# Split weights in one tile, the odd tiles of the contraction 128 bytes further, activations at one distance behind them

## The chip, the core and the metric

The kernel runs on one core of a Trainium2 chip. The time is device microseconds from launch to end; the kernel before takes 1659.15 us (median of three runs, 1659.05 to 1659.46). A core has a matrix engine (PE, TensorE) that reads its operands from on-chip memory (SBUF, 128 partitions wide) and adds its products up in PSUM; DVE (VectorE) and ACT (ScalarE) for elementwise work; POOL (GpSimd); and SP, which here issues the weight loads. Each engine runs its own list of instructions in order. Engines wait for one another on semaphores: an instruction counts one up when it is done, and another instruction is held until the count has reached a number.

## What is computed

One inference step of a decoder layer, for 256 prompt tokens and 8 x 4 sample tokens together, 288 columns. Cut to what matters here, it is a row of products of the tokens with large float32 weights:

```
proj = x @ w_in                        # 2048 -> 11280 columns
y_a  = (gB * conv3(gC * h)) @ w_a_out  # short convolution mixer
y_b  = gated_delta_rule(q, k, v, g, beta) normalised, * silu(z), @ w_b_out
x    = layer_norm(ALPHA * x + (sig(m_a) * y_a + sig(m_b) * y_b) @ w_o)
hid  = square(relu(x @ w_up))          # 2048 -> 8192
x    = layer_norm(ALPHA * x + hid @ w_down)
```

The outputs are the new x of both groups of tokens and the new states of the two convolutions and of the delta rule.

## The kernel before

Float32 products are made out of three matmuls of a shorter format (`float32r`): a weight w is split into `hi` = w rounded and `lo` = w - hi, the activations likewise, and PE adds up hi x hi, hi x lo and lo x hi.

All weights stream from memory in **blocks** of 512 KB: KB = 4 tiles of the contraction (k, 128 rows each) by GW = 256 columns, in SBUF 4096 bytes a partition. There are 496. Block i goes through four steps:

- `load(i)` (L167): SP fetches it into a `raw` buffer;
- `split_hi(i)` (L183): one ACT cast raw -> `hi`, 1024 elements a partition, line L187;
- `split_lo(i)` (L189): one DVE subtraction raw - hi -> `lo`, recorded under L142, the line of the helper `tt`;
- `matmuls(i)` (L196): for each of the four k, six matmuls of 288 columns: both 128-column halves c of `hi` with the high and the low activations (L219), then both halves of `lo` with the high activations (L221); 24 in a block.

`raw`, `hi` and `lo` come from a pool of four buffers each (L114), each buffer a tile of its own. The loop over the blocks (L1643 to L1734) writes the instructions out in a fixed order; nothing is reordered afterwards. From block 10 on, one turn of it is: `split_hi(i + 3)`, side work (a step of the delta rule up to the merge), `split_lo(i + 3)`, whatever falls due for finished groups (`due`, evacuations from PSUM), `matmuls(i)`, and the load of block i + 7. With four buffers, block i + 3 takes the buffers of block i - 1, so its cast must wait until PE has made its last `hi` matmul of block i - 1 and its subtraction until the last `lo` matmul; blocks i, i + 1 and i + 2 are split by then.

The activations lie in tiles of 16 rows (k) per partition, 288 float32 each, 1152 bytes from row to row: `xh`, `xl` for the input, `hh`, `hl` for the hidden layer, `ahl`, `mh`, `ml` for the mixers. `dh` and `dl`, the input of the up projection, have NX = 290 columns in a row, 1160 bytes, and `ohl` is allocated so too.

Taken from the built program, a weight tile before always starts 128 bytes past a multiple of 256, whichever k it is; an activation row of 1152 bytes starts in the same place for even k and 128 bytes from it for odd k, and the rows of `dh` and `dl` wander in steps of 136 bytes modulo 256.

Of the kernel before, what the change touches and what calls it, by code (L numbers as in the profile page):

```python
# [10 lines left out]
F32R = mybir.dt.float32r  # L11
# [5 lines left out]
P = 128  # L17
# [2 lines left out]
NS = 32  # L20
NT = NP_ + NS
NX = NT + 2
KT = D // P
H = 8
DFF = 8192
# [8 lines left out]
GW = 256  # L34
KB = 4
# [70 lines left out]
def hybrid_kernel(ctx: ExitStack, tc: tile.TileContext, A):  # L106
# [7 lines left out]
    wp = pool("wp", 4)  # L114
# [7 lines left out]
    def nm(s):  # L122
        counter[0] += 1
        return f"{s}{counter[0]}"
# [16 lines left out]
    def tt(out, a, b, op):  # L141
        dve.tensor_tensor(out=out, in0=a, in1=b, op=op)  # L142
# [8 lines left out]
    blocks = []  # L151
# [5 lines left out]
            blocks.append((gi, row0 + j * kb * P, j * kb, j == 0, j == nk // kb - 1))  # L157

    raw, his, los = {}, {}, {}
    due = {}  # L160
    fill = []

# [19 lines left out]

    def split_hi(i, step=KB):  # L183
        if i < len(blocks):
            his[i] = wp.tile([P, KB, GW], F32R, tag="hi", name=nm("hi"))
            for k in range(0, KB, step):
                act.copy(his[i][:, k:k + step], raw[i][:, k:k + step])  # L187

    def split_lo(i, step=KB):  # L189
        if i < len(blocks):  # L190
            los[i] = wp.tile([P, KB, GW], F32R, tag="lo", name=nm("lo"))
            r = raw[i] if blocks[i][0].get("by_token") else raw.pop(i)
            for k in range(0, KB, step):
                tt(los[i][:, k:k + step], r[:, k:k + step], his[i][:, k:k + step], SUB)

    def matmuls(i):  # L196
        gi, r0, k0, first, last = blocks[i]
        if gi.get("by_token"):
            return first_tokens(i, k0)
# [9 lines left out]
        h, l = (u.rearrange("p k c -> p (k c)").rearrange("p (k c) -> p k c", k=kb) for u in (h, l))  # L209
        for k in range(kb):  # L210
            xh_, xl_ = ah[:, k0 + k, 0:n], al[:, k0 + k, 0:n]
            st = first and k == 0
            en = last and k == kb - 1
            per = gi["cols"] // P // len(members)
            for u, m in enumerate(members):
                ts = [(m["ps"][:, t, 0:n], slice((per * u + t) * P, (per * u + t + 1) * P)) for t in range(per)]
                both = [(o, c, x) for o, c in ts for x in (xh_, xl_)]
                for o, c, x in both[::2] + both[1::2] if i == 0 else both:
                    pe.matmul(o, h[:, k, c], x, start=st and x is xh_, stop=False)  # L219
                for o, c in ts:  # L220
                    pe.matmul(o, l[:, k, c], xh_, start=False, stop=en)  # L221
# [12 lines left out]
    ph = {}  # L234
# [11 lines left out]
    ident = cst("ident")  # L246
    ones = cst("ones")

    xh = xp.tile([P, KT, NT], F32R, tag="XH", name="xh")
    xl = xp.tile([P, KT, NT], F32R, tag="XL", name="xl")  # L250
    hw = cp.tile([P, 24, 28], F32, name="hw")
# [165 lines left out]
    def wo_evac(p):  # L417
        q = slice(2 * p, 2 * p + 2)

        def resid(ps):  # L420
            pl = ph["pool"]
            if p == 0:
                ph["dl"] = pl.tile([P, KT, NX], F32R, tag="R3", name="dl")
                ph["dh"] = pl.tile([P, KT, NX], F32R, tag="R4", name="dh")
                t = ap_.tile([P, 2, H, NT], F32, tag="ao", name="lns").rearrange("p a h t -> p (a h) t")
                ph["qa"], ph["da"], ph["c"] = t[:, 0:2], t[:, 2:4], t[:, 4]
                ph["ln"] = [t[:, 5 + u] for u in range(4)]
                dh, dl = ph["dh"], ph["dl"]
                gbc = lnp[:, 0:32].rearrange("p (a k) -> p k a", a=2)
                act.copy(hmr, ones)  # L430
                act.copy(dh[:, :, NT:NX], gbc)
                tt(dl[:, :, NT:NX], gbc, dh[:, :, NT:NX], SUB)
            ph["s"] = pl.tile([P, 2, NT], F32, tag="yt", name=nm("s"), bufs=2)
            dd = ph["s"]
            stt(dd, xh[:, q, :], ALPHA, ps[:, :, 0:NT], MUL, ADD)
            stt(dd, xl[:, q, :], ALPHA, dd, MUL, ADD)
            if p:
                tt(dd, dd, bmid(ph["c"], 2), SUB)

        def centre(ps):  # L440
            tt(ph["c"], ph["s"][:, 0, :], ph["s"][:, 1, :], ADD)
            ph["chl"] = high_low(ph["c"], "sg")

        def shift(ps):
            cps = gtile()
            dd = ph["s"]
            row_sums(cps[:, 0:NT], ph["chl"])
            act.mul(ph["c"], cps[:, 0:NT], 1.0 / 256)
            tt(dd, dd, bmid(ph["c"], 2), SUB)

        def scaled(ps):
            dd, qa, da = ph["s"], ph["qa"], ph["da"]
            sd = ph["pool"].tile([P, 2, NT], F32, tag="sg", name=nm("sd"), bufs=2)
            for u in range(2):
                k = 2 * p + u
                dve.tensor_scalar(out=sd[:, u, :], in0=dd[:, u, :], scalar1=lnp[:, k:k + 1], scalar2=None, op0=MUL)
            act.copy(ph["dh"][:, q, 0:NT], sd)
            tt(ph["dl"][:, q, 0:NT], sd, ph["dh"][:, q, 0:NT], SUB)

        def sums(ps):  # L460
            dd, qa, da = ph["s"], ph["qa"], ph["da"]
            if p == 0:
                act.activation(qa, dd, AF.Square)
                act.copy(da, dd)
# [267 lines left out]
    def products(out, b, j, ks=range(KB)):  # L732
        h, l = kept[j]
        c = slice(b * P, b * P + P)
        for k in ks:
            kk = KB * j + k
            en = kk == KT - 1
            for x, w, stop in ((ph["hh"], h, False), (ph["hh"], l, False), (ph["hl"], h, en)):
                pe.matmul(out, x[:, kk, c], w[:, k, :], start=False, stop=stop)  # L739

    def first_tokens(i, k0):
        kept.append((his.pop(i), los.pop(i)))
# [849 lines left out]
    aux = []  # L1592
    steps = x_steps(0, 1)
    t0, o0 = steps[0]()
    his[0] = wp.tile([P, KB, GW], F32R, tag="hi", name=nm("hi"))
    los[0] = wp.tile([P, KB, GW], F32R, tag="lo", name=nm("lo"))
    t, h0, l0 = raw.pop(0), his[0], los[0]

    def split_first(k):
        for u in (2 * k, 2 * k + 1):  # L1600
            act.copy(h0[:, u], t[:, u])  # L1601
            tt(l0[:, u], t[:, u], h0[:, u], SUB)

    def turns(ts):
        for g in ts:
# [14 lines left out]
    turns(t0[0:2])  # L1620
    xs_out = x_sample(0)
    warm_up(1, 2)
    act.copy(h0[:, 0], t[:, 0])
    o0[0](dve.tensor_copy)
    xs_out()
    tt(l0[:, 0], t[:, 0], h0[:, 0], SUB)
    act.copy(h0[:, 1], t[:, 1])
    tt(l0[:, 1], t[:, 1], h0[:, 1], SUB)
# [14 lines left out]
    for i in range(len(blocks)):  # L1643
# [48 lines left out]
        if i == mark["merge"]:  # L1692
            gcm.__exit__(None, None, None)
            p3 = pool("p3")
            ph["pool"] = p3
            r1 = p3.tile([P, KT, NT], F32R, tag="R1", name="ahl")
            r4 = p3.tile([P, KT, NX], F32R, tag="R4", name="ohl")
            ph["mg"] = p3.tile([P, KT, NX], F32, tag="R3", name="mg")[:, :, 0:NT]

            def halves(key, r, src):  # L1700
                for q in range(2):
                    s = slice(4 * q, 4 * q + 4)
                    s8 = slice(8 + 4 * q, 12 + 4 * q)
# [64 lines left out]
```

## Time and profile before

| | |
|---|---|
| median of the runs | 1659.15 us |
| span of the profiled execution, first to last instruction | 1656.8 us |
| what lies around it, as the difference of the two | 2.35 us |
| PE busy | 1648.6 us, 100% |
| DVE busy | 981.5 us, 59% |
| ACT busy | 786.0 us, 47% |
| DMA | 280.42 MB, 169 GB/s |

The page lists no time of the profiled execution beside its span; the median stands for it here. A busy PE in this profile means that a matmul was in flight, from its start to its modelled end, so matmuls that follow one another closely read as 100% however close they are: what counts for their rate is the time from one start to the next. In a list by time, a row gives the start and the length in us, engine, line, operation, output and inputs, and in brackets how long the engine had stood still and who released it.

### The profile page before, as it was taken

What the parts mean: (1) busy time and instruction counts of PE and PEld (TensorE: products, weight loads), DVE (VectorE), ACT (ScalarE), POOL (GpSimd) and SP (SyncE); (2) the same over time, 40 slices, a digit from 0 to 9 for tenths busy, and PEclk for the clock granted to TensorE, in tenths of its full rate; (3) what the DMA queues carried; (4) which work ended last, traced back from release to release, by engine and by line L of the source; (5) the groups of instructions that cost most, each with busy time, mean ns of one, the idle gap of its engine ahead of it and who ended that gap; (6) DMA issues with size and microseconds to landing.
All of it is one profiled execution on the core that took longest, in us unless ns stands there. A gap on an engine that the chain in (4) does not pass through costs nothing.

```text
span 1656.8 us, 31402 instructions
## 1 busy us (share of the span) xinstructions
PE 1648.6 (100%) x13130; PEld 1633.9 (99%) x13130; DVE 981.5 (59%) x1299; ACT 786.0 (47%) x1231; POOL 139.1 (8%) x273
## 2 busy tenths in 40 slices
PE   9999999999999999999999999999999999999998
PEld 8999999999999999999999999999999999999998
DVE  6788688767544444457776666444444444444466
ACT  6786756448533333334444455443334433344354
POOL 1142216133000000000000000000000000000011
PEclk9999999999999999999999999999999999999999
DMA  8555456545555555555565555555555555555552
GB/s 272 177 168 170 137 173 203 183 130 175 186 168 165 166 165 166 165 165 159 166 218 165 166 166 165 166 166 166 165 166 166 166 166 165 166 165 166 179 163 100
DMA packets 273237, 280.42 MB, mean 169 GB/s; under 512 B 13728, under 2 KB 267221, under 8 KB 272833
## 3 DMA queue, kind: packets, MB, share of 16 engines
q1 hardware_dynamic: 269190, 266.06, 51.5%
q0 software_dynamic: 3616, 12.02, 2.5%
q8 instruction: 103, 1.69, 0.4%
q10 hardware_dynamic: 288, 0.33, 0.1%
q14 instruction: 40, 0.32, 0.1%
HBM read 270.88 MB, written 7.48 MB: 168 GB/s over the span
## 4 chain that ended last, share of the span: by engine, by line
PE 98%; DVE 1%; ACT 1%; DMA 0%; issue 0%; SPq 0%; ACTq 0%
PE acc L219 62%; PE acc L221 31%; PE acc L739 1%; PE g L1327 0%; PE g L1499 0%; PE g L1519 0%; PE g L1522 0%; DMA raw<-in_w_in_dram 0%; PE g L1318 0%; PE g L1219 0%; PE g L1477 0%; DVE lo L142 0%; PE g L1511 0%; DVE w L145 0%; ACT hi L187 0%
## 5 line engine op out<-in xcount | busy, mean ns | idle before, releaser
L142 DVE TENSOR_TENSOR lo<-raw,hi 128x1024 fp32r<-128x1024 f32 (+1 forms) x503 | 607.3, 1211 | 576.8 <-ACT hi L187 575.0
L187 ACT CAST hi<-raw 128x1024 fp32r<-128x1024 f32 (+1 forms) x499 | 519.0, 1043 | 729.2 <-PE acc L219 659.1
L219 PE MATMUL acc<-xh,hi 128*128 128x288 f32 x1408 | 397.9, 298 | 1.0 <-ACT hi L1601 0.5
L219 PE MATMUL acc<-xl,hi 128*128 128x288 f32 x1408 | 394.2, 295 | 0.0
L221 PE MATMUL acc<-xh,lo 128*128 128x288 f32 x1408 | 302.6, 296 | 0.2 <-DVE lo L142 0.2
L219 PE MATMUL acc<-dl,hi 128*128 128x288 f32 (+1 forms) x1024 | 287.7, 295 | 0.0
L219 PE MATMUL acc<-dh,hi 128*128 128x288 f32 (+1 forms) x1024 | 287.4, 295 | 0.0
L219 PE MATMUL acc<-hl,hi 128*128 128x288 f32 x992 | 277.8, 295 | 0.0
L219 PE MATMUL acc<-hh,hi 128*128 128x288 f32 x992 | 277.4, 294 | 0.0
L219 PEld LDWEIGHTS acc<-xh,hi 128*128 128x128 f32 x1408 | 264.3, 188 | 3.8 <-issue 1.6
L219 PEld LDWEIGHTS acc<-xl,hi 128*128 128x128 f32 x1408 | 264.2, 188 | 1.0 <-DVE xl L142 0.2
L221 PEld LDWEIGHTS acc<-xh,lo 128*128 128x128 f32 x1408 | 226.0, 188 | 0.7 <-DVE lo L142 0.6
L221 PE MATMUL acc<-dh,lo 128*128 128x288 f32 (+1 forms) x1024 | 219.8, 296 | 0.0
L221 PE MATMUL acc<-hh,lo 128*128 128x288 f32 x992 | 213.2, 296 | 0.0
L219 PEld LDWEIGHTS acc<-dh,hi 128*128 128x128 f32 x1024 | 193.3, 189 | 0.0
L219 PEld LDWEIGHTS acc<-dl,hi 128*128 128x128 f32 x1024 | 192.8, 188 | 0.0
L219 PEld LDWEIGHTS acc<-hh,hi 128*128 128x128 f32 x992 | 186.4, 188 | 0.4 <-issue 0.4
L219 PEld LDWEIGHTS acc<-hl,hi 128*128 128x128 f32 x992 | 186.1, 188 | 0.0
L221 PEld LDWEIGHTS acc<-dh,lo 128*128 128x128 f32 x1024 | 164.5, 188 | 0.0
L221 PEld LDWEIGHTS acc<-hh,lo 128*128 128x128 f32 x992 | 159.0, 188 | 0.0
L219 PE MATMUL acc<-mh,hi 128*128 128x288 f32 x256 | 71.9, 297 | 0.0
L219 PE MATMUL acc<-ml,hi 128*128 128x288 f32 x256 | 71.7, 295 | 0.0
(423 smaller groups left out, 1489.3 us busy)
## 6 DMA issues: line engine op xcount, KB each, us to landing
raw<-in_w_in_dram SPq DMA_DIRECT2D x175, 512.0 KB, 3.5
raw<-in_w_up_dram SPq DMA_DIRECT2D x128, 512.0 KB, 3.6
raw<-in_w_down_dram SPq DMA_DIRECT2D x128, 512.0 KB, 3.6
raw<-in_w_o_dram SPq DMA_DIRECT2D x32, 512.0 KB, 4.0
raw<-in_w_a_out_dram SPq DMA_DIRECT2D x16, 512.0 KB, 3.6
raw<-in_w_b_out_dram SPq DMA_DIRECT2D x16, 512.0 KB, 3.6
S<-in_state_gdn_dram POOLq DMA_DIRECT2D x8, 512.0 KB, 5.7
out_dram<-S POOLq DMA_DIRECT2D x8, 512.0 KB, 4.7
```

The costliest lines, as they stand in the source:

```text
L142: dve.tensor_tensor(out=out, in0=a, in1=b, op=op)
L187: act.copy(his[i][:, k:k + step], raw[i][:, k:k + step])
L219: pe.matmul(o, h[:, k, c], x, start=st and x is xh_, stop=False)
L221: pe.matmul(o, l[:, k, c], xh_, start=False, stop=en)
L739: pe.matmul(out, x[:, kk, c], w[:, k, :], start=False, stop=stop)
```

## The change

Three things are moved, and no arithmetic is.

**The split weights** are no longer eight tiles (four `hi`, four `lo`) but pieces of one, `wsplit`, of 8296 elements a partition. It has two halves, WODD = 4128 elements (16,512 bytes) apart. Buffer b (i modulo 4) has 1024 elements in each half: 512 for `hi` and 512 for `lo`. Of a block's four k the two even ones stand in the first half, the two odd ones in the second, and 16,512 is 128 more than a multiple of 256. So the cast and the subtraction of a block each write two stretches of 2048 bytes with 14 KB between them, in which pieces of the other three buffers lie.

**The activations** get rows that are all alike: `dh` and `dl` have 352 columns in a row (1408 bytes), `ohl` 288.

**The reads** follow (`matmuls`, `products`). In the built program each activation row now stands 144 bytes past its weight tile modulo 256, for every k and every stage.

```diff
+NXS = 352
...
+    WBUF, WSHIFT, WODD = 4, 4, 4 * 1024 + 32
+    wsplit = []
+
+    def weight_halves(i):
+        if not wsplit:
+            arena = wp.tile([P, 8296], F32R, tag="split", name="wsplit", bufs=1)
+            wsplit.append(arena[:, WSHIFT:WSHIFT + 2 * WODD].rearrange("p (r c) -> p r c", r=2))
+        b = 1024 * (i % WBUF)
+        return [wsplit[0][:, :, b + o:b + o + 512].rearrange("p r (u c) -> p r u c", u=2) for o in (0, 512)]
+
+    def by_parity(t, i):
+        return t.rearrange("p (u r) c -> p r u c" if blocks[i][0]["kb"] == KB else "p (r u) c -> p r u c", r=2)
+
+    def split_parts(i, step):
+        if step == KB:
+            return [(slice(None), slice(None))]
...
     def split_hi(i, step=KB):
         if i < len(blocks):
-            his[i] = wp.tile([P, KB, GW], F32R, tag="hi", name=nm("hi"))
-            for k in range(0, KB, step):
-                act.copy(his[i][:, k:k + step], raw[i][:, k:k + step])
+            his[i] = weight_halves(i)[0]
+            r = by_parity(raw[i], i)
+            for a, b in split_parts(i, step):
+                act.copy(his[i][:, a, b], r[:, a, b])
 
     def split_lo(i, step=KB):
         if i < len(blocks):
-            los[i] = wp.tile([P, KB, GW], F32R, tag="lo", name=nm("lo"))
-            r = raw[i] if blocks[i][0].get("by_token") else raw.pop(i)
-            for k in range(0, KB, step):
-                tt(los[i][:, k:k + step], r[:, k:k + step], his[i][:, k:k + step], SUB)
+            los[i] = weight_halves(i)[1]
+            r = by_parity(raw[i] if blocks[i][0].get("by_token") else raw.pop(i), i)
+            for a, b in split_parts(i, step):
+                tt(los[i][:, a, b], r[:, a, b], his[i][:, a, b], SUB)
...
-                    pe.matmul(o, h[:, k, c], x, start=st and x is xh_, stop=False)
+                    pe.matmul(o, h[k][:, c], x, start=st and x is xh_, stop=False)
...
-                    pe.matmul(o, l[:, k, c], xh_, start=False, stop=en)
+                    pe.matmul(o, l[k][:, c], xh_, start=False, stop=en)
...
-                ph["dl"] = pl.tile([P, KT, NX], F32R, tag="R3", name="dl")
-                ph["dh"] = pl.tile([P, KT, NX], F32R, tag="R4", name="dh")
+                ph["dl"] = pl.tile([P, KT, NXS], F32R, tag="R3", name="dl")[:, :, 0:NX]
+                ph["dh"] = pl.tile([P, KT, NXS], F32R, tag="R4", name="dh")[:, :, 0:NX]
...
-            r4 = p3.tile([P, KT, NX], F32R, tag="R4", name="ohl")
+            r4 = p3.tile([P, KT, NT], F32R, tag="R4", name="ohl")
```

The order of the work on every engine stays as it was. What the built program changes besides the addresses is who waits for whom. The place shown is the second block of a group of the up projection (output `acc`, activations `dh` and `dl`). First PE, before: the last matmuls of the block ahead, and the first k and more of this one.

```order
L219 MATMUL acc_11894<-dl,hi_11794 128x288
L221 MATMUL acc_11894<-dh,lo_11796 128x288 x2
L219 MATMUL acc_11894<-dh,hi_11824 128x288 [waits Activation_49]
L219 MATMUL acc_11894<-dl,hi_11824 128x288
L219 MATMUL acc_11894<-dh,hi_11824 128x288
L219 MATMUL acc_11894<-dl,hi_11824 128x288
L221 MATMUL acc_11894<-dh,lo_11826 128x288 [waits DVE_49]
L221 MATMUL acc_11894<-dh,lo_11826 128x288
```

The block waits for its own cast (`hi_11824`) at its first matmul and for its own subtraction (`lo_11826`) at its first `lo`. PE at the same place, now:

```order
L242 MATMUL acc_11271<-dl,wsplit 128x288
L244 MATMUL acc_11271<-dh,wsplit 128x288 x2
L242 MATMUL acc_11271<-dh,wsplit 128x288 [waits DVE_49]
L242 MATMUL acc_11271<-dl,wsplit 128x288
L242 MATMUL acc_11271<-dh,wsplit 128x288
L242 MATMUL acc_11271<-dl,wsplit 128x288
L244 MATMUL acc_11271<-dh,wsplit 128x288 x2
```

The wait on ACT and the wait of the first `lo` are gone; in place of both, the block's first matmul waits for a count of DVE's. Which DVE instruction that is shows DVE's own list at this place, now (the block's own raw buffer is `raw_11114`, those of the three blocks behind it are `raw_11145`, `raw_11177` and `raw_11205`; `r` is an evacuation):

```order
L143 TENSOR_TENSOR wsplit<-raw_11114,wsplit 128x2x512 [waits DMAHW5_49,PE_49,Activation_49]
L143 TENSOR_TENSOR wsplit<-raw_11145,wsplit 128x2x512 [waits DMAHW6_49,PE_49,Activation_49]
L143 TENSOR_TENSOR wsplit<-raw_11177,wsplit 128x2x512 [waits DMAHW7_49,PE_49,Activation_49]
L143 TENSOR_TENSOR r_11268<-r_11267 128x576 [waits Activation_49]
L143 TENSOR_TENSOR wsplit<-raw_11205,wsplit 128x2x512 [waits DMAHW0_49,PE_49,Activation_49]
```

The number in PE's wait is that of the last of these rows, the `lo` of the block three further on (i + 3), and no longer that of the first. That subtraction in turn waits, as before, for PE's last `lo` matmul of block i - 1 and for ACT's cast of block i + 3, which waits for PE's last `hi` matmul of block i - 1. It is so in every block from the sixth on with i modulo 4 = 1, 2 or 3; where i modulo 4 is 0, the wait stands at the first matmul of the second k, six matmuls later. (The stretch from a write's first to its last byte covers the pieces that these matmuls read; the bytes that it writes are not theirs.)

More of the change, by code (lines that the diff above doesn't have):

```diff
@@ L159, in hybrid_kernel @@
     raw, his, los = {}, {}, {}
+    WBUF, WSHIFT, WODD = 4, 4, 4 * 1024 + 32
[11 more added lines that the diff above has]
+            return [(slice(None), slice(None))]
+        wide = blocks[i][0]["kb"] < KB
+        if step == 2:
+            return [(k, slice(None)) if wide else (slice(None), k) for k in range(2)]
+        return [(k // 2, k % 2) if wide else (k % 2, k // 2) for k in range(KB)]
     due = {}
@@ L208, in matmuls @@
         kb = gi["kb"]
-        h, l = (u.rearrange("p k c -> p (k c)").rearrange("p (k c) -> p k c", k=kb) for u in (h, l))
+        h, l = ([u[:, k % 2, k // 2] for k in range(KB)] if kb == KB else
+                [u[:, k].rearrange("p u c -> p (u c)") for k in range(2)] for u in (h, l))
         for k in range(kb):
@@ L247, in hybrid_kernel @@
     ones = cst("ones")
+    weight_halves(0)
     xh = xp.tile([P, KT, NT], F32R, tag="XH", name="xh")
@@ L738, in products @@
             for x, w, stop in ((ph["hh"], h, False), (ph["hh"], l, False), (ph["hl"], h, en)):
-                pe.matmul(out, x[:, kk, c], w[:, k, :], start=False, stop=stop)
+                pe.matmul(out, x[:, kk, c], w[:, k % 2, k // 2], start=False, stop=stop)
     def first_tokens(i, k0):
@@ L1594, in hybrid_kernel @@
     t0, o0 = steps[0]()
-    his[0] = wp.tile([P, KB, GW], F32R, tag="hi", name=nm("hi"))
-    los[0] = wp.tile([P, KB, GW], F32R, tag="lo", name=nm("lo"))
-    t, h0, l0 = raw.pop(0), his[0], los[0]
+    his[0], los[0] = weight_halves(0)
+    t = raw.pop(0)
+    h0, l0 = ([u[:, k // 2, k % 2] for k in range(KB)] for u in (his[0], los[0]))
     def split_first(k):
         for u in (2 * k, 2 * k + 1):
-            act.copy(h0[:, u], t[:, u])
-            tt(l0[:, u], t[:, u], h0[:, u], SUB)
+            act.copy(h0[u], t[:, u])
+            tt(l0[u], t[:, u], h0[u], SUB)
     def turns(ts):
@@ L1622, in hybrid_kernel @@
     warm_up(1, 2)
-    act.copy(h0[:, 0], t[:, 0])
+    act.copy(h0[0], t[:, 0])
     o0[0](dve.tensor_copy)
     xs_out()
-    tt(l0[:, 0], t[:, 0], h0[:, 0], SUB)
-    act.copy(h0[:, 1], t[:, 1])
-    tt(l0[:, 1], t[:, 1], h0[:, 1], SUB)
+    tt(l0[0], t[:, 0], h0[0], SUB)
+    act.copy(h0[1], t[:, 1])
+    tt(l0[1], t[:, 1], h0[1], SUB)
     fill.extend([second_tile, idle, idle, idle, second_half])
```

## The prediction

> **What bounds the kernel now.** First the page: the span, the share of PE, the chain of waits by engine.
>
> ```profile
> span 1656.8 us, 31402 instructions
> ...
> PE 98%; DVE 1%; ACT 1%; DMA 0%; issue 0%; SPq 0%; ACTq 0%
> ```
>
> The chain is PE's own queue. How close its matmuls follow one another, the windows view tells, for a stretch of up and down projections:
>
> ```profile
> core 0: us, PE busy (x) PEld busy (x) DVE busy (x) ACT busy (x) POOL busy (x), PEclk, DMA share, GB/s
> 1300.00:1500.00 200.00, 200.00 (x1506) 200.00 (x1506) 92.38 (x87) 75.19 (x79) 0.00 (x0) 1.00 0.53 165
> ```
>
> 200 us over 1506 matmuls is 0.1328 us each at the full granted clock, 0.797 us for the six of one k, 3.19 us for a block of 24. DVE and ACT stand still half the time. How far they run ahead, the list of waits and the groups by form show:
>
> ```profile
> ACT hi L187 <- PE acc L219: 659.1, 347, 4.0
> DVE lo L142 <- ACT hi L187: 575.0, 362, 4.1
> ```
>
> ```profile
> L142 DVE TENSOR_TENSOR lo<-raw,hi 128x1024 fp32r<-128x1024 f32 x493 | 603.1, 1225 | 576.3 <-ACT hi L187 575.0 <-PE acc L221 0.3
> L187 ACT CAST hi<-raw 128x1024 fp32r<-128x1024 f32 x493 | 516.7, 1049 | 729.2 <-PE acc L219 659.1 <-issue 60.3 <-ACT hi L187 8.0
> ```
>
> So in 347 of 493 blocks the cast stands ready until PE lets go of a buffer, and the subtraction follows it at once. This loop from PE over ACT to DVE is closed once a block already; it costs nothing, because what it makes is read only three blocks later. The list by time shows one turn:
>
> ```profile
> 1303.55 0.30 PE L219 MATMUL acc<-dl,hi 128*128 128x288 f32 x1
> 1303.69 0.42 PE L221 MATMUL acc<-dh,lo 128*128 128x288 f32 x2
> 1303.89 1.05 ACT L187 CAST hi<-raw 128x1024 fp32r<-128x1024 f32 x1 [1.55 <-PE acc L219]
> 1303.95 0.30 PE L219 MATMUL acc<-dh,hi 128*128 128x288 f32 x1
> ...
> 1304.75 0.29 PE L219 MATMUL acc<-dh,hi 128*128 128x288 f32 x1
> ...
> 1304.97 1.23 DVE L142 TENSOR_TENSOR lo<-raw,hi 128x1024 fp32r<-128x1024 f32 x1 [1.26 <-ACT hi L187]
> ...
> 1305.56 0.29 PE L219 MATMUL acc<-dh,hi 128*128 128x288 f32 x1
> ...
> 1306.34 0.29 PE L219 MATMUL acc<-dh,hi 128*128 128x288 f32 x1
> ...
> 1307.15 0.29 PE L219 MATMUL acc<-dh,hi 128*128 128x288 f32 x1
> ```
>
> The last `hi` matmul of block i - 1 starts at 1303.55; that releases the cast for block i + 3, at 1303.89; the subtraction ends at 1304.97 + 1.23 = 1306.20. PE began block i at 1303.95, with no gap.
>
> **The change part by part.** *The wait.* By the built program, the first matmul of block i (i modulo 4 = 1, 2, 3) now waits for the `lo` of block i + 3, that is for the instruction that here ends at 1306.20. Everything behind it on PE stands too: the 24 matmuls, the group's end for which ACT and DVE evacuate, and the next cast. The slack of three blocks is gone and the loop is on the path. What PE needs after a release, the start of the kernel shows:
>
> ```profile
> 4.46 0.53 PE L219 MATMUL acc<-xh,hi 128*128 128x288 f32 x2 [0.41 <-ACT xh L945]
> 4.81 0.75 DVE L142 TENSOR_TENSOR lo<-raw,hi 128x256 fp32r<-128x256 f32 x2
> ...
> 5.28 0.19 PEld L221 LDWEIGHTS acc<-xh,lo 128*128 128x128 f32 x1
> ```
>
> The first of two subtractions of 0.375 us ends at 5.19, the weight load that needs it starts at 5.28: 0.1 us. And two matmuls behind a wait take 0.53 us where a pair in the stream takes 0.42: 0.1 us to start again. So block i starts at 1306.30 instead of 1303.95, 2.35 us late, and with the restart loses 2.45 us. Where i modulo 4 is 0, the wait stands at the second k, which would start at 1304.75: 1306.30 - 1304.75 = 1.55, and 1.65 with the restart. Four blocks lose 3 x 2.45 + 1.65 = 9.0 us, a block 2.25 us.
>
> Of the 493 full-size subtractions some 486 stand between a block and its predecessor in this way (blocks 6 on): 486 x 2.25 = **1094 us**.
>
> *Side work.* In the other 146 blocks (493 - 347) the cast did not wait for PE last, ACT or DVE being busy with evacuations or the delta rule; there the loop closes later still. The price lies between nothing, since a block that lasts 5.4 us instead of 3.2 leaves these engines more room, and one evacuation of some 1 us in each, 146 us. I take 0.2 us each, **30 us**, near nothing for that reason.
>
> *The shape of the copies.* Cast and subtraction read and write pieces instead of 1024 elements in a row. The rows to compare are a cast of two rows of 256 out of one instruction, and two casts of 256:
>
> ```profile
> 7.50 0.71 ACT L1601 CAST hi<-raw 128x256 fp32r<-128x256 f32 x2 [0.51 <-DMA raw<-in_w_in_dram]
> ```
>
> ```profile
> 19.45 0.59 ACT L962 CAST xh<-g 128x512 fp32r<-128x512 f32 x1 [2.17 <-PE g L956]
> ```
>
> Two instructions take 0.71, one with two pieces 0.59; between 0.355 for 256 and 1.049 for 1024, a line gives 0.59 for 512. Pieces cost nothing, and I take **0**; if each of four pieces cost as much as an instruction of its own, it would be 4 x 0.355 - 1.049 = 0.37 on ACT and 4 x 0.375 - 1.225 = 0.28 on DVE, 0.65 a block or 316 us, since both are now on the path.
>
> *The addresses.* In the list by time the k from 1304.75 take 0.81, 0.78 and 0.81 us for the same six matmuls; only the place of the activation row to the weights differs among these k. So places matter, by some 2% either way. No row has a distance of 144 for all six matmuls. Bounds: all 1968 steps (492 blocks of four) at 0.78 would give 1968 x (0.78 - 0.797) = -33 us, all at 0.81, +26 us; a gap to the unknown best as wide as the spread twice over, 0.06 a step, -118 us. I take **0**, the mean of the places seen. The Trainium skill, "TensorE: Matmul & The Clock Gate", Part 2, step 1 of "Step-by-step: what each phase is for", says that streaming operand and weight load have independent read ports and the one takes no bandwidth from the other; by that rule placing is worth nothing here and this term is 0 exactly. The spread of the three k speaks against it.
>
> Loads need no term: `load(i + 7)` waits for the same subtraction as before and has three blocks, now longer ones, to land.
>
> *Sum:* 1094 + 30 = 1124 us. The profiled execution has a span of 1656.8 us and 2.35 us around it by the median of 1659.15: 1659 + 1124 = 2783, said as **2780 us**.
>
> **The rivals.** *The clock falls.* PE would stand 2.45 us in every 5.6. The tail of this trace shows the granted clock go down:
>
> ```profile
> 1649.00:1652.40 3.40, 2.23 (x13) 1.30 (x11) 2.94 (x8) 1.77 (x5) 0.00 (x0) 1.00 0.37 140
> 1652.40:1656.70 4.30, 0.00 (x0) 0.00 (x0) 0.00 (x0) 0.24 (x1) 0.00 (x0) 0.50 0.61 228
> ```
>
> It is 1.00 while PE is busy for 2.23 of 3.40 us and 0.50 in the 4.30 us with no matmul. At half clock a block's matmuls take another 3.19 us: 492 x 3.19 = 1569, the whole 4350 us if it stays down, about 3300 if a third of the time. For it: the share of 2.23 in 3.40 is near what is coming (3.19 in 5.5), and none lower is seen at full clock. Against it: full idleness is what it took. The Trainium skill, "TensorE: Matmul & The Clock Gate", section "Why this matters for your kernels", asks for no gaps over about 3 us between bursts of matmuls; by that rule gaps of 2.45 leave the clock up, and the rows do not contradict it. Chance 0.12.
>
> *The pieces cost.* 2783 + 316 = 3100 us; against it stands the 0.59 row. Chance 0.06.
>
> *Faster: the wait is met in time and the distance pays.* If that `lo` were done before block i - 1 ends, PE would run without a gap, and 144 bytes everywhere would decide: 1659 - 33 = 1626 us. It decides at 1303.95: the subtraction would have to end 2.25 us sooner than in the list by time. It cannot be hurried by addresses, since its cast waits for PE's own last `hi` matmul; only a wait on another instruction than I read would do it. Chance 0.04. *The change does nothing*, the wait met and the distance worthless: 1659 us, chance 0.02.
>
> **How the numbers follow.** The forecast, with the full clock, has 0.76. Its own range: lower end 1659 + 1094 - 118 = 2635, without side work and with the widest gain by address; upper end 2783 + 26 + 116 (side work at its dearest) = 2925. To reach 8 in 10 I go up to 3080, which takes in most of the case with dear pieces and the clock down for a tenth of the time (157 us): 2630 to 3080. Faster by over 0.2% has 0.04, within 0.2%, about what a measurement of this kernel can tell from no change, 0.02, slower 0.94.
>
> **What would show it.** In the profile after: PE's busy share near 60%; idle time of PE some 1.1 ms, nearly all ahead of the `hi` matmuls and released by DVE's subtraction into `wsplit`, about 486 times, the longest group near 2.3 us; the chain of waits going round PE, ACT and DVE; blocks in a pattern of four, three full gaps and a shorter one behind the first six matmuls. The granted clock 1.00 and cast and subtraction still 1.05 and 1.23 us would clear the two slower rivals. The time between matmul starts inside a k gives the address term alone: 0.133 for no effect, under 0.130 for a gain. Wrong I would be if PE shows no gaps (then I misread the wait), or if the gaps are there and PE's clock is 0.5.

## The result and the profile after

The changed kernel takes 3065.76 us (median of four runs, 3060.9 to 3075.45); the kernel before, run beside it, 1659.31 us. The ratio is 1.848, with an interval of 1.845 to 1.851. The profiled execution has a span of 3059.0 us.

The page of the changed kernel, the same lines as before (L242 is now the line of the `hi` matmuls, L244 that of the `lo` matmuls, L209 the cast, L143 the helper of the subtraction):

```profile
span 3059.0 us, 31319 instructions
...
PE 2074.8 (68%) x13130; PEld 1948.3 (64%) x13130; DVE 987.6 (32%) x1299; ACT 789.5 (26%) x1231; POOL 116.5 (4%) x273
...
PEclk8789888998888898889888988888888898898888
...
PE 44%; DVE 16%; ACT 13%; issue 2%; ACTq 0%; DVEq 0%
...
L143 DVE TENSOR_TENSOR wsplit<-raw,wsplit 128x1024 fp32r<-128x1024 f32 (+1 forms) x503 | 608.3, 1210 | 1824.6 <-ACT wsplit L209 1824.0
L209 ACT CAST wsplit<-raw 128x1024 fp32r<-128x1024 f32 (+1 forms) x499 | 518.4, 1040 | 2135.8 <-PE acc L242 2099.8
```

DVE and ACT do the same work in the same time as before: 1.21 and 1.04 us an instruction (before: 1.211 and 1.043). What is new is in three lines. The chain of waits, which was PE at 98%, now goes round PE, DVE and ACT. PE is busy for 68%. And its granted clock, which stood at full speed, is 0.7 to 0.9 in every slice. The list of waits of the changed kernel (total in us, times, the longest) names the releaser:

```profile
ACT wsplit L209 <- PE acc L242: 2099.8, 465, 8.3
DVE wsplit L143 <- ACT wsplit L209: 1824.0, 442, 8.0
...
PE acc L242 <- DVE wsplit L143: 968.9, 487, 7.0
```

The first two waits were there before and cost nothing then. The third is the one that closes the loop: 487 times PE stands until a subtraction is done, 2.0 us on average. The list by time of the changed kernel shows turns of it:

```profile
2504.22 0.43 PE L244 MATMUL acc<-hh,wsplit 128*128 128x288 f32 x2
2504.41 1.04 ACT L209 CAST wsplit<-raw 128x1024 fp32r<-128x1024 f32 x1 [6.01 <-PE acc L242]
2505.49 1.22 DVE L143 TENSOR_TENSOR wsplit<-raw,wsplit 128x1024 fp32r<-128x1024 f32 x1 [5.83 <-ACT wsplit L209]
...
2506.77 0.40 PE L242 MATMUL acc<-hh,wsplit 128*128 128x288 f32 x1 [2.13 <-DVE wsplit L143]
```

```profile
2512.32 0.40 PE L242 MATMUL acc<-hh,wsplit 128*128 128x288 f32 x1 [1.35 <-DVE wsplit L143]
...
2517.10 0.40 PE L242 MATMUL acc<-hh,wsplit 128*128 128x288 f32 x1 [2.14 <-DVE wsplit L143]
...
2522.65 0.40 PE L242 MATMUL acc<-hh,wsplit 128*128 128x288 f32 x1 [2.14 <-DVE wsplit L143]
...
2524.98 0.44 PE L242 MATMUL acc<-hh,wsplit 128*128 128x288 f32 x1
...
2526.42 0.44 PE L242 MATMUL acc<-hh,wsplit 128*128 128x288 f32 x1
```

PE ends block i - 1, ACT casts for block i + 3, DVE subtracts, and 0.06 us after that PE may begin block i. Gaps of 2.13 and 2.14 us, and a shorter one of 1.35 behind the first k of every fourth block. The last two rows are the starts of two neighbouring k: 1.44 us apart, where a k took about 0.79 before. That is the other half of the story. Windows cut where the recorded clock of this kernel changes (2523.53, 2526.94, 2530.35 us; columns as in the windows quoted before: PE busy first, the granted clock the third number from the end):

```profile
2516.70:2520.11 3.41, 3.01 (x23) 3.01 (x24) 0.34 (x1) 0.00 (x0) 0.00 (x0) 1.00 0.46 154
2520.11:2523.53 3.42, 1.28 (x10) 1.06 (x9) 1.22 (x1) 1.04 (x1) 0.00 (x0) 1.00 0.01 2
2523.53:2526.94 3.41, 3.41 (x17) 3.41 (x16) 0.00 (x0) 0.00 (x0) 0.00 (x0) 0.50 0.53 154
2526.94:2530.35 3.41, 1.28 (x9) 1.04 (x9) 1.23 (x1) 1.04 (x1) 0.00 (x0) 1.00 0.00 0
2530.35:2533.77 3.42, 3.42 (x17) 3.42 (x16) 0.00 (x0) 0.00 (x0) 0.00 (x0) 0.50 0.52 158
```

Twice PE is busy for 1.28 of 3.41 us, and twice the next 3.41 us run at clock 0.50, full of matmuls that take almost twice as long. The view of the clock by core gives what this adds up to:

```profile
core 0: 3059.0 us, clock 0.881
```

With 1.00 and 0.50 as the only levels, a mean of 0.881 means (1 - 0.881) / 0.5 x 3059 = 728 us at half clock.

### The profile page after: what moved, and what is told of

It reads as the page before. It is cut to its first block, busy times and chain, and to the rows that moved or that the text cites. A ratio compares the mean times of both kernels' runs of the same rounds, so it can differ in the third digit from the quotient of the medians.

```text
span 3059.0 us, 31319 instructions
## 1 busy us (share of the span) xinstructions
PE 2074.8 (68%) x13130; PEld 1948.3 (64%) x13130; DVE 987.6 (32%) x1299; ACT 789.5 (26%) x1231; POOL 116.5 (4%) x273
## 3 DMA queue, kind: packets, MB, share of 16 engines
q8 instruction: 102, 1.67, 0.3%
## 4 chain that ended last, share of the span: by engine, by line
PE 44%; DVE 16%; ACT 13%; issue 2%; ACTq 0%; DVEq 0%
PE acc L242 33%; DVE wsplit L143 15%; ACT wsplit L209 13%; PE acc L244 11%; PE acc L763 0%; DVE s L146 0%; DVE lns L532 0%; DVE lns L143 0%; DVE dl L143 0%; ACT dh L481 0%; DVE sd L480 0%; DVE Y L146 0%; ACT Y L876 0%; ACT Y L690 0%; DVE lns L146 0%
## 5 line engine op out<-in xcount | busy, mean ns | idle before, releaser
L143 DVE TENSOR_TENSOR wsplit<-raw,wsplit 128x1024 fp32r<-128x1024 f32 (+1 forms) x503 | 608.3, 1210 | 1824.6 <-ACT wsplit L209 1824.0
L209 ACT CAST wsplit<-raw 128x1024 fp32r<-128x1024 f32 (+1 forms) x499 | 518.4, 1040 | 2135.8 <-PE acc L242 2099.8
L242 PE MATMUL acc<-xh,wsplit 128*128 128x288 f32 x1408 | 472.3, 347 | 359.4 <-DVE wsplit L143 352.3
L242 PEld LDWEIGHTS acc<-xh,wsplit 128*128 128x128 f32 x1408 | 315.0, 224 | 402.0 <-DVE wsplit L143 357.4
L242 PE MATMUL acc<-dh,wsplit 128*128 128x288 f32 (+1 forms) x1024 | 343.0, 346 | 252.9 <-DVE wsplit L143 252.9
L242 PE MATMUL acc<-hh,wsplit 128*128 128x288 f32 x992 | 329.1, 344 | 238.8 <-DVE wsplit L143 238.8
L242 PE MATMUL acc<-xl,wsplit 128*128 128x288 f32 x1408 | 449.9, 331 | 0.0
L242 PEld LDWEIGHTS acc<-dh,wsplit 128*128 128x128 f32 x1024 | 229.6, 224 | 282.6 <-DVE wsplit L143 282.6
L242 PEld LDWEIGHTS acc<-hh,wsplit 128*128 128x128 f32 x992 | 220.3, 222 | 267.6 <-DVE wsplit L143 267.6
L244 PE MATMUL acc<-xh,wsplit 128*128 128x288 f32 x1408 | 344.4, 330 | 0.0
L242 PE MATMUL acc<-dl,wsplit 128*128 128x288 f32 (+1 forms) x1024 | 326.9, 331 | 0.0
L242 PEld LDWEIGHTS acc<-xl,wsplit 128*128 128x128 f32 x1408 | 315.8, 224 | 0.5 <-DVE xl L143 0.3
L242 PE MATMUL acc<-hl,wsplit 128*128 128x288 f32 x992 | 313.3, 328 | 0.0
L244 PEld LDWEIGHTS acc<-xh,wsplit 128*128 128x128 f32 x1408 | 269.3, 224 | 0.2 <-DVE wsplit L143 0.2
L244 PE MATMUL acc<-dh,wsplit 128*128 128x288 f32 (+1 forms) x1024 | 248.5, 328 | 0.0
L244 PE MATMUL acc<-hh,wsplit 128*128 128x288 f32 x992 | 238.8, 326 | 0.0
L242 PEld LDWEIGHTS acc<-dl,wsplit 128*128 128x128 f32 x1024 | 229.4, 224 | 0.0
L242 PEld LDWEIGHTS acc<-hl,wsplit 128*128 128x128 f32 x992 | 220.1, 222 | 0.0
L244 PEld LDWEIGHTS acc<-dh,wsplit 128*128 128x128 f32 x1024 | 193.5, 221 | 0.0
L244 PEld LDWEIGHTS acc<-hh,wsplit 128*128 128x128 f32 x992 | 185.5, 219 | 0.0
L242 PE MATMUL acc<-mh,wsplit 128*128 128x288 f32 x256 | 84.7, 343 | 62.8 <-DVE wsplit L143 62.8
L242 PEld LDWEIGHTS acc<-mh,wsplit 128*128 128x128 f32 x256 | 56.6, 221 | 70.2 <-DVE wsplit L143 70.2
```

The costliest lines, as they stand in the source:

```text
L209: act.copy(his[i][:, a, b], r[:, a, b])
L242: pe.matmul(o, h[k][:, c], x, start=st and x is xh_, stop=False)
L244: pe.matmul(o, l[k][:, c], xh_, start=False, stop=en)
```

## The experiments

The theory at the start: the early waits make the gaps, the gaps make the clock fall, and the new places themselves cost nothing. Rivals: the places slow PE down; the clock has another cause; the copies in pieces are dear. Times are medians, ratios are to the kernel before on the same chip. "Distance as before" means that it changes from k to k as in the kernel before.

| run | early waits | distance modulo 256 | us | ratio, interval |
|---|---|---|---|---|
| changed kernel | yes | 144 | 3065.8 | 1.848, 1.845 to 1.851 |
| e1_two_pieces | no | 144 | 1642.2 | 0.990, 0.988 to 0.991 |
| e2_old_places | no | as before | 1660.0 | 1.000, 0.999 to 1.001 |
| e3_filled | yes, gaps filled | 144 | 2831.3 | one run |
| e4_pairs | no | 144 | 1643.0 | 0.990, 0.988 to 0.991 |
| e5_longer_tile | no | 144 | 1643.4 | 0.990, 0.989 to 0.992 |
| e6_spare_words | yes | as before | 3078.6 | 1.855, 1.851 to 1.858 |
| e7_at_0 | no | 0 | 1654.8 | 0.997, 0.996 to 0.998 |
| e8_at_128 | no | 128 | 1660.2 | 1.000, 0.999 to 1.001 |
| e9_fill_10 | yes, gaps half filled | 144 | 2846.1 | one run |
| e10_fill_4 | yes, gaps filled a little | 144 | 3069.9 | one run |
| e11_at_240 | no | 240 | 1656.9 | 0.998, 0.997 to 0.999 |
| e12_at_160 | no | 160 | 1660.0 | 1.000, 0.999 to 1.001 |

### Two instructions in place of one

```diff
         if step == KB:
-            return [(slice(None), slice(None))]
+            return [(0, slice(None)), (1, slice(None))]
```

> The changed kernel, but cast and subtraction are issued once for each of the two halves of the tile (512 elements each) and no longer as one instruction that reaches over both. Addresses and distances are those of the changed kernel. Theory (the added time is the wait for the subtraction three blocks ahead, and the clock that falls in the gaps it makes): no instruction writes over another block's weights any more, so the gaps and the clock's fall go together: PE 98% of the chain, clock 1.00, and what is left is the effect of the addresses, 131.7 ns between matmul starts in the changed kernel at full clock against 132.75 before, over 13130 matmuls at most -14 us: 1645 to 1655 us. Rival (the interleaved places themselves make PE or the copies slow): still above 2900 us. Rival (only the pieces are dear): between, since two instructions of 512 take 0.59 + 0.59 on ACT instead of 1.04, hidden if PE does not wait.

Measured 1642.2 us, a little below the expected range. The span, the chain and the copies of this kernel:

```profile
span 1641.3 us, 33184 instructions
...
PE 98%; DVE 1%; DMA 0%; issue 0%; ACT 0%; SPq 0%; DVEq 0%
```

```profile
L143 DVE TENSOR_TENSOR wsplit<-raw,wsplit 128x512 fp32r<-128x512 f32 x988 | 671.4, 694 | 491.1 <-ACT wsplit L209 453.6 <-PE acc L242 3.5
L209 ACT CAST wsplit<-raw 128x512 fp32r<-128x512 f32 x988 | 602.7, 621 | 637.3 <-PE acc L242 580.3 <-issue 36.0 <-ACT wsplit L209 11.7
```

The places and distances of the changed kernel are all there, with 493 more instructions on ACT and on DVE, and the whole loss of 1400 us is gone. So neither the places nor the interleaved tile slow anything on the chip. The copies cost more in this form (two of 621 ns for one of 1040) and it does not matter, since they are off the path again.

### One instruction, other lengths and groups

```diff
-    WBUF, WSHIFT, WODD = 4, 4, 4 * 1024 + 32
+    WBUF, WSHIFT, WODD = 4, 0, 4 * 1024
...
-            arena = wp.tile([P, 8296], F32R, tag="split", name="wsplit", bufs=1)
+            arena = wp.tile([P, 8192], F32R, tag="split", name="wsplit", bufs=1)
```

(and the activation rows of `dh`, `dl` and `ohl` as before the change)

> The changed kernel with one tile and one instruction for both halves as it is, but with the places of before: no 128 bytes between even and odd, no 144 bytes to the activations. Theory (waits and clock, not places): the waits stay, so 3066 us within 1%, some 487 waits of PE for the subtraction of 2.1 us and more, clock near 0.88. Rival (the new distance is what costs): it falls back toward 1659 us. If the distance gains what the starts inside a k say (131.7 against 132.75 ns), this kernel is 10 to 15 us slower than the changed one.

Measured 1660.0 us: the expectation failed. The list of waits of this kernel has the waits of ACT and DVE as before the change, and no wait of PE for a subtraction but one of 0.3 us:

```profile
ACT wsplit L209 <- PE acc L242: 659.8, 348, 4.0
DVE wsplit L143 <- ACT wsplit L209: 573.8, 361, 4.1
```

It had been taken for granted that one instruction over both halves, with other buffers between them, is enough to bring the early wait. It is not. In the built program of this kernel a block waits for its own cast and its own subtraction, though the two halves are 16,384 bytes apart and the buffers interleave just so. What differs from the changed kernel, beside the places, is that the two halves fill the tile exactly. Since places and waits both went back, this run could not say which of them mattered; the next two runs separate them. e5_longer_tile keeps the distance of 144 and makes the tile eight elements longer, with the pieces eight elements (32 bytes) further into it:

```diff
-    WBUF, WSHIFT, WODD = 4, 4, 4 * 1024 + 32
+    WBUF, WSHIFT, WODD = 4, 12, 4 * 1024 + 32
...
-            arena = wp.tile([P, 8296], F32R, tag="split", name="wsplit", bufs=1)
+            arena = wp.tile([P, 8304], F32R, tag="split", name="wsplit", bufs=1)
```

> The changed kernel with a tile of 8304 elements in place of 8296, and the pieces 8 elements further into it, so that the distance to the activations is 144 again (the weights themselves stand 32 bytes further on modulo 256). In the built program the early waits are gone with that: the first matmul of a block waits for its own cast, the first lo for its own subtraction, as before the change. Theory (the waits, which hang on the length of the tile, are the whole loss, and the clock falls only because of them): 1642 us, as with two instructions or two groups. Rival (two pieces in four buffers that interleave, 14 KB apart, cost something on the chip itself): over 1660, up to 3066 us.

1643.4 us. Eight more unused elements take 1422 us off the changed kernel. e6_spare_words starts from e2_old_places and adds eight unused elements at the front:

```diff
-    WBUF, WSHIFT, WODD = 4, 0, 4 * 1024
+    WBUF, WSHIFT, WODD = 4, 8, 4 * 1024
...
-            arena = wp.tile([P, 8192], F32R, tag="split", name="wsplit", bufs=1)
+            arena = wp.tile([P, 8200], F32R, tag="split", name="wsplit", bufs=1)
```

> The kernel with the places of before (1660.0 us), and 8 unused elements ahead of the pieces: the tile has 8200 elements instead of 8192, every distance between weights and activations stays. In the built program this brings the early waits back. Theory (it is the waits alone): about 3080 us, the 3066 of the changed kernel and some 17 more for the places of before, PE waiting some 487 times for a subtraction, clock near 0.88. Rival (the loss needs the new places, 128 bytes between even and odd or 144 bytes to the activations): near 1660 us.

3078.6 us, with the distances of before. Page and waits of this kernel:

```profile
span 3079.8 us, 31319 instructions
```

```profile
PE acc L242 <- DVE wsplit L143: 966.5, 486, 7.0
```

The same wait, 486 times, without a byte between even and odd. So the loss hangs on what the built program waits for and on nothing else of the change. Which lengths bring the early waits can be read from built programs without running them: with elements to spare, 8200, 8264 and 8296 bring them, 8208, 8224, 8240, 8288 and 8304, all multiples of 16, do not; and 8200 does not either when it is two halves of 4100 that fill it. The rule behind this was not found.

A fourth way keeps a long tile with spare elements (8360, again no multiple of 16) and sorts the buffers instead, even blocks in one stretch of the tile, odd ones in the next, so that blocks i and i + 3 never share a stretch:

```diff
-    WBUF, WSHIFT, WODD = 4, 4, 4 * 1024 + 32
+    WSHIFT, WODD = 4, 2 * 1024 + 32
...
-            arena = wp.tile([P, 8296], F32R, tag="split", name="wsplit", bufs=1)
+            arena = wp.tile([P, 8360], F32R, tag="split", name="wsplit", bufs=1)
...
+            for q in range(2):
+                o = WSHIFT + 2 * WODD * q
+                wsplit.append(arena[:, o:o + 2 * WODD].rearrange("p (r c) -> p r c", r=2))
+        b = 1024 * (i // 2 % 2)
```

> The changed kernel with one instruction for both halves, but with the four buffers in two groups: blocks of even number in one stretch of the tile, blocks of odd number in the next. The subtraction three blocks ahead then writes in the other stretch than the block that PE is about to read; only the one two blocks ahead lies in the same, and that is ready a block sooner. Distances and addresses modulo 256 as in the changed kernel. Theory (the stretch from first to last byte makes the wait): gaps gone, clock 1.00, 1645 to 1655 us like the kernel with two instructions. Rival (an instruction that writes both halves is dear by itself, by its pieces): clearly slower than that one. If the wait two blocks ahead is also late, gaps of at most the short kind, 1900 us or more.

1643.0 us, with one instruction of two pieces for each copy (and, to make room, one small tile elsewhere that shares another's place); e1, e4 and e5 agree within 1.2 us.

### The clock

e3_filled keeps the early waits and puts products of a zero tile into the gaps, from the merge on (before 800 us of the program):

```diff
+            if i >= mark["merge"] and k == (0 if i % 4 else 1):
+                new = first and k == 0
+                for _ in range(18 if i % 4 else 11):
+                    pe.matmul(ps[:, 0, 0:P], ph["wz"], ph["wz"], start=new, stop=new)
```

e9_fill_10 and e10_fill_4 put 10 and 4 such products into each full gap and none into the short one.

> The changed kernel with products of a zero weight tile added ahead of the weights that PE waits for, from the second stage of the program on: 18 matmuls of 128 columns ahead of a block, 11 ahead of the second k of each fourth block. They add nothing to the sums and do not wait for the subtraction, so they run inside the gap. Theory (a part of the added time is the clock, halved for 732 of 3059 us in the trace of the changed kernel, which falls because PE is idle in the gaps): the clock stays at 1.00 where they run, and the time falls by some 200 us, to about 2850 (2800 to 2900), although PE has more to do. Rival (the clock falls for another reason, heat or work, or is no part of the cost): the clock stays near 0.88 or falls further, and the time is 3060 or more.

> The kernel with filled gaps, but only 10 products of the zero tile ahead of a block (18 of them took 2.12 us there, so 10 take some 1.2) and none in the short gap: about 0.95 us of each full gap stays idle. They add nothing to the sums. Theory (the clock goes down where PE is busy for less than about 0.4 of some 3.4 us, and a gap of 2.13 us leaves (3.4 - 2.13) / 3.4 = 0.37): a gap of 0.95 leaves 0.72, so the clock stays at 1.00 after the merge and the time is that of the fully filled kernel, 2831 us, within 20. Rival (any gap of about 1 us lowers the clock for a while, in proportion): half way, 2920 to 2980 us, clock 0.93 to 0.97 after the merge.

> The same with 4 products of the zero tile in each full gap: 4 x 0.118 = 0.47 us filled, 1.66 us idle, and 1.35 us in the short gap. Theory (a bound between 0.37 and about 0.45 of busy time): (3.4 - 1.66) / 3.4 = 0.51 is over it, so the clock stays at 1.00 after the merge all the same and the time is 2831 us within 20. Rival (in proportion to the idle time): 1.66 of 2.13 us idle, so about three quarters of the clock's loss stay: about 3000 us, clock near 0.91 after the merge.

Measured 2831.3, 2846.1 and 3069.9 us. A stretch behind the merge, in the order: changed kernel, e3_filled, e9_fill_10, e10_fill_4.

```profile
2000.00:2400.00 400.00, 270.31 (x1615) 254.90 (x1615) 99.42 (x93) 80.17 (x85) 0.00 (x0) 0.89 0.29 88
```

```profile
2000.00:2400.00 400.00, 386.59 (x3005) 375.93 (x3005) 109.92 (x102) 86.94 (x91) 0.00 (x0) 1.00 0.32 98
```

```profile
2000.00:2400.00 400.00, 315.19 (x2355) 302.99 (x2353) 108.72 (x101) 87.57 (x91) 0.00 (x0) 1.00 0.32 99
```

```profile
2000.00:2400.00 400.00, 290.30 (x1807) 279.60 (x1808) 98.65 (x92) 78.49 (x83) 0.00 (x0) 0.88 0.28 88
```

With 18 or 10 products in a gap the clock is 1.00 and the kernel is 234 and 220 us faster, though PE has some 6000 or 3000 matmuls more to do and waits for the same subtraction. So a part of the loss is the clock, and the clock falls because PE stands idle, not because it works. With four products nothing is gained, neither clock nor time: here the expectation failed, and so did the rival of a loss in proportion. The list by time of e9_fill_10 and that of e10_fill_4 show how little separates the two:

```profile
2500.89 1.23 PE L237 MATMUL acc<-wz 128*128 128x128 f32 x10
2503.20 0.40 PE L246 MATMUL acc<-dh,wsplit 128*128 128x288 f32 x1 [1.08 <-DVE wsplit L143]
```

```profile
2512.68 0.56 PE L237 MATMUL acc<-wz 128*128 128x128 f32 x4
2514.98 0.40 PE L246 MATMUL acc<-hh,wsplit 128*128 128x288 f32 x1 [1.74 <-DVE wsplit L143]
```

Idle times of 1.08 us, and of 1.35 in the short gaps that e9_fill_10 leaves empty, let the clock stand; 1.74 us lowers it as surely as 2.14. Windows of e10_fill_4, again cut at the changes of its clock:

```profile
2505.68:2509.09 3.41, 2.01 (x17) 1.86 (x15) 0.94 (x1) 1.05 (x1) 0.00 (x0) 1.00 0.28 98
2509.09:2512.51 3.42, 3.08 (x23) 3.08 (x24) 0.28 (x1) 0.00 (x0) 0.00 (x0) 1.00 0.48 153
2512.51:2515.92 3.41, 1.67 (x14) 1.53 (x13) 1.22 (x1) 1.05 (x1) 0.00 (x0) 1.00 0.00 0
2515.92:2519.33 3.41, 3.41 (x16) 3.41 (x16) 0.00 (x0) 0.00 (x0) 0.00 (x0) 0.50 0.56 156
2519.33:2522.75 3.42, 2.08 (x16) 1.85 (x15) 1.89 (x2) 1.05 (x1) 0.00 (x0) 1.00 0.01 3
```

Here 2.01 us of work in 3.41 keep the clock up, 1.67 do not. The gap of 1.74 us that ends at 2509.43 is cut by a border, 1.40 us in the first row and 0.34 in the second, and does no harm; the one that ends at 2514.98 lies within the third row, and the fourth runs at half clock. So these rows read as a matter of phase between a loop of 5.6 us and windows of 3.41, which would be why only some of the gaps cost clock.

### The distance

The three kernels at 144 gain 17 us on the kernel before, so the distance has a price of its own. Four kernels have one other distance everywhere, without early waits. Their edit, with WSHIFT 0, 32, 4 and 24 for the distances 0, 128, 240 and 160:

```diff
-            arena = wp.tile([P, 8296], F32R, tag="split", name="wsplit", bufs=1)
-            wsplit.append(arena[:, WSHIFT:WSHIFT + 2 * WODD].rearrange("p (r c) -> p r c", r=2))
-        b = 1024 * (i % WBUF)
+            arena = wp.tile([P, 2 * WODD], F32R, tag="split", name="wsplit", bufs=1)
+            wsplit.append(arena.rearrange("p (r c) -> p r c", r=2))
+        b = WSHIFT + 1024 * (i % WBUF)
```

> Distance 0 instead of 144 for every k and stage, without early waits (tile of two whole halves of 4128 elements, even and odd 128 bytes apart as in the change). Theory (the gain of 17 us is that no k stands at 128 any more, where a k of the trace before takes 802.4 ns; at 0 it takes 790.8, at 144 786.7): 1968 k at 4 ns more than at 144, 1642 + 8 = 1650 us. Rival (144 itself is what helps): near 1659 us or above. Rival (distance is worth nothing once all are alike): 1642 us.

> Distance 128 for every k and stage, without early waits, otherwise as the kernel with distance 0. Theory (the places set the rate of the matmuls, k by k, as in the trace before): 802.4 ns a k against 786.7 at 144, 1968 x 15.7 ns = 31 us more, 1673 us, slower than before the change. Rival (what counts is that all are alike, or the 128 bytes between even and odd): 1642 to 1650 us.

> Distance 240 instead of 144 for every k and stage, without early waits; the weights stand at the addresses modulo 256 that they have in the changed kernel. 0 and 128 gave 1654.8 and 1660.2, 144 gives 1642 to 1643. Theory (a distance that is an odd multiple of 16 is the good kind, one that is a multiple of 32 the other): 1642 us, 786.7 ns a k. Rival (144 is a place of its own): 1655 to 1660 us, 796.7 ns a k.

> Distance 160 for every k and stage, without early waits. Theory (a multiple of 32 is the slower kind): 1655 to 1660 us, 796.7 ns a k. Rival (the further from 0 and 128 the better, 144 and 160 alike): 1642 us. Rival (neither): something between or outside, which would leave the rule of distance open.

Measured 1654.8, 1660.2, 1656.9 and 1660.0 us. At 128 the theory failed by 13 us, at 0 by 5, and the guess of odd multiples of 16 fell at 240; the rival by which 144 is a place of its own is what came there, and 160 came out as slow as its theory said. The stretch of up and down projections of e5_longer_tile (144) and of e8_at_128:

```profile
1300.00:1500.00 200.00, 200.00 (x1528) 200.00 (x1527) 94.44 (x88) 75.33 (x80) 0.00 (x0) 1.00 0.55 168
```

```profile
1300.00:1500.00 200.00, 200.00 (x1508) 200.00 (x1507) 93.22 (x87) 74.42 (x80) 0.00 (x0) 1.00 0.54 166
```

Six matmuls take 200 / 1528 x 6 = 0.785 us at 144 and 0.796 at 128; before the change, where the distance changes from k to k, it was 0.797 with 1506. Distances 0, 240 and 160 have 1509, 1511 and 1509 matmuls here. So in this stretch all distances tried but 144 stay within 0.4% of the rate of before, and 144 is 1.4% faster (1528 / 1506 = 1.0146). The 802.4 and 790.8 ns of the single k, from which the expectations were worked out, average 796.6: what one k lost there its neighbour gained, and such times of single steps do not price a distance that all have. In the down projection, where these two times come from, a k takes 796.7 ns both in the kernel at 0 and in the one at 128. Why 144 is better stays open; it is better in e5 too, where the weights stand 32 bytes further on.

## Why the prediction was right, and where it was off

**What bounds, and that the slack was nothing to lean on.** Right: the loop PE, ACT, DVE, which closed once a block before at no cost, is now on the path, as the chain of 44, 16 and 13% says.

**The wait, 1094 us.** Right in place, count and size. It names 486 blocks; the list of waits has 487. From 2517.10 to 2522.65 are 5.55 us for a block, of which four k at 0.787 us (1642-us kernels: 0.785 in the windows, 0.787 over all its k) take 3.15: 2.40 us lost, where 2.45 was said. From 2506.77 to 2512.32 are 5.55 us for five k: 1.61 lost, where 1.65 was said. Four blocks lose 3 x 2.40 + 1.61 = 8.81, in 487 blocks 1073 us. The signs named for it, 1.1 ms of idle time and a busy share near 60%, came as 968.9 us and 68%: the restart and the longer matmuls at half clock count as busy.

**Side work and copies, 30 and 0 us.** The copies keep 1.21 and 1.04 us: right, and that rival fell. Side work is what remains in the sum below, 21 us or somewhat more.

**Addresses, 0 us.** Off by 17 us to the good side, within the bounds of -118 to +26. The rule weighed there (the Trainium skill, "TensorE: Matmul & The Clock Gate", Part 2, independent read ports for streaming operand and weight load) would have made it exactly nothing; 1643.4 us at 144 against 1660.0 at 160 with the same waits, instructions and clock speak against that. Whether the ports are the reason, no run shows.

**The clock, 0 us: this is the step that failed.** The forecast took the full clock, and left the fall to a rival with a chance of 0.12. Its reason was that "full idleness is what it took" in the tail of the trace; 2.13 us of idle time in a window of 3.41 are enough. That reason also read the tail from the wrong row. In the windows of the changed kernel the row at 0.50 is full of matmuls, and it is the row before it that lacked them. Read in the same order, the clock in the tail fell after the row with 2.23 us of work in 3.40, and the 4.30 us without a matmul came once it was down. The Trainium skill, same page, "Why this matters for your kernels", asks for no gap over about 3 us; by that rule these gaps are harmless. The runs show otherwise: idle times of 2.14 us, and of 1.74, lower the clock again and again. Nor did the rival have the size. It put a block at half clock at another 3.19 us, twice the time, and reckoned with a third of the time or all of it. A k at half clock takes 1.44 us against 0.787, so 45% of that time is lost; and most falls (186 of 198) last one window of 3.41 us, after which PE, busy for nearly all of it, has its clock back. 728 us at half clock cost at most 728 x (1.44 - 0.787) / 1.44 = 330 us.

**The sum again.** 1659 - 17 + 330 leaves 3066 - 1972 = 1094 us for the gaps, of which 1073 are the waits counted above; 21 are left for the side work, or somewhat more, since 330 is a bound. The list of waits gives the gaps without sample turns: 968.9 us of idle time in 487 waits, each of which costs about 0.26 us more than its idle time (2.40 lost, 2.14 idle), another 127 us, so 1096 together. The fillers give a check that does not use the 1094. e9_fill_10 shows a mean clock of 0.957 over 2844.2 us, so 245 us at half clock in place of 728; (728 - 245) x 0.453 = 219 us less than 3066 is 2847, and 2846.1 was measured. The same working gives 2823 for e3_filled (0.966 over 2829.3 us; measured 2831.3) and 3067 for e10_fill_4 (0.881 over 3067.9; measured 3069.9).

**The range** of 2630 to 3080 holds the time by luck. It had been stretched for dear pieces and for a clock that is down for a tenth of the time (157 us), not for one that costs up to 330. With the clock and the addresses at their measured price, the forecast's own terms would have made 2783 + 330 - 17 = 3096, above the range; the waits and the side work came out about 30 us cheaper. What the prediction would have called itself wrong about, gaps with a clock of 0.5, is what came, for a quarter of the time.

**The rival on the other side**, 1626 us if the wait were met and the distance paid, was no idle thought: without the early waits the change is worth 17 us, 1642 us, about half of the 33 reckoned at the best. The early wait was never a property of the places.

## What to carry over

When buffers that were tiles of their own become pieces of one tile, look in the built program at which instruction the first reader now waits for, and try a tile that its halves fill exactly, or one instruction for each piece: here eight unused elements decided between 1643 and 3066 us. A loop that runs a block ahead at no cost shows its full length, here 2.4 us a block, when a wait is moved to its latest instruction. And gaps on PE cost more than their length: count those of 1.7 us and more in a trace like this, and try the fix of the waits before any filler, which gave back 234 us of 1400.

## What the runs showed of the hardware

- The granted clock has two levels here, 1.00 and 0.50, and it changes at points that are multiples of 3.41 us apart. A window in which PE was busy for 1.28 or 1.67 of 3.41 us was followed by one at 0.50, one with 2.01 was not. In the changed kernel 195 of the 198 windows before a fall have PE busy at most 0.45 of the time, by the union of its matmul records, and the 483 full-speed windows that another one followed at least 0.44. The exact measure is open: with four zero products in the gap the usual share before a fall is 0.49, and in the tail of the kernel before, among other matmuls, the clock fell after 2.23 of 3.40 us, 0.66.
- At half clock matmul starts lie 0.24 us apart (a k in 1.44 us), at full clock 0.131: not quite a factor of two, 1.83.
- Products of 128 columns with a weight load each follow one another at 0.11 us, by the rows of 10 and of 4 shown above: (1.23 - 0.56) / 6. Those of 288 columns do at 0.13, so less than half the columns save 15% of the time.
- The place of activations to weights modulo 256 goes with 1.4% of PE's rate in that stretch at 144, and with 0.1 to 0.4% at 0, 128, 160 and 240. Places were compared modulo 256 only, so another modulus is not ruled out.
